# Preparation of the products of a block-wise up-projection rearranged: weight sums, taps, operands, kept tiles, transfers

## The chip, the core and the metric

The kernel runs on one core of a Trainium2 chip. The metric is the device time of one execution in microseconds (us); a kernel's time is the median of three executions. The engines are named as in the profile: PE (TensorE, matmuls), DVE (VectorE), ACT (ScalarE), POOL (GpSimd), SP (SyncE, which issues the DMA transfers). Each engine takes its instructions in the order in which the program lists them, and semaphores make one wait for another.

## The reference

One layer of a decoder for 1024 prompt positions and 8 decoded ones (1032 columns), model width 1024, feed-forward width 2816. What the change touches is the end of the mixer, the gated feed-forward block and the start of its down-projection:

```python
    x = x + m @ w_out                                   # m: merged branches
    h = rmsnorm(x, g_ffn)
    up = causal_dwconv(h @ w_up, buf, conv_f_w, conv_f_b)   # width 3, per channel
    gate, val = up[..., :D_FF], up[..., D_FF:]
    x = x + (jax.nn.gelu(gate) * val) @ w_down
```

Everything is float32; the kernel writes each matmul operand as a rounded part and a remainder (fp32r) and adds three products of such parts.

## The kernel before, in words

All activations lie with channels on the 128 partitions and the 1032 positions along the free axis. A weight tile of 128 output channels comes from memory into a `raw` or `val` tile; ACT casts it to the rounded part and DVE subtracts that from the source to get the remainder. The stage that the change touches is a list of 186 jobs, run by `run_jobs`. A job is one PE product (`product`, L1072): 24 matmuls of 128x128 by 258 columns, which is half of the contraction (four tiles of 128) for half of the positions (516 columns), three part products each.

- **Out-projection**: 32 jobs, `out_job`, two position halves times eight output tiles times two contraction halves. After each output tile DVE adds the product to x (L1124), ACT squares it (L1128), DVE adds the squares up (L1130). At the end of each half `stats` and `factors` make the norm's factor with a few small matmuls (L250, L279).
- **Up-projection**: 154 jobs, `up_job`. Gate and value channels of one row i (22 rows), split in halves of the contraction, are multiplied by the four quarters of h in seven products instead of eight: kinds m, r, p, c, q, b, z. Kinds r, p, c, q multiply sums of weight quarters; DVE makes a sum (L1243) right before ACT's cast (L973) and DVE's remainder (L978). The activations' operands are sums too: b11, b21, t1, t2, b22, t3, t4, each four tiles, made by `operand` from the normed h (norm L1167, differences L1175 and L1177, cast L235, remainder L236). Product m of row i, then p, q and z, add into one PSUM tile; r and c share another; between two of them `done` reads the intermediate value out (m L1263 or L1265, r L1267, p L1269, c L1271, q L1273, b L1275, z L1277). The b products of rows 0 to 9 come first, while the second half's operands are not there yet; in rows 2 to 9 the order is m of row i, z of row i-1, then r, p, c, q of row i. From row 10 on it is m, r, p, c, q, b, z.
- **After z**: `finish_up` convolves both halves of the row: a first tap on ACT (L1291), two taps on DVE (L1288, twice), gelu on ACT (L1309), the product of the two on DVE (L1313), and the result goes to memory (`actd`). These steps stand in `queue`.

`run_jobs` sets the order of all that, written out by the program itself (no scheduler moves it): for job n it issues the matmuls, then `done` of job n-1, then ACT's cast for job n+3 (`LOOK` = 3, `prep_hi`), then what hangs on the job, then steps from `queue` as long as the budget is positive (`SLOT` = 2.7 us less the costs, `drain`), then DVE's remainder for job n+3 (`prep_lo`), after which the next weight transfer is issued. At the end of the list the first eight results come back from memory (`fetch_act`) and are taken apart (ACT L1350, DVE L1351) for the down-projection, whose matmuls are those of `gemm` (L231).

All 16 tiles of x for the out-projection, the convolution's state and two packed weight tiles are asked for from SP before the first job.

## Time and profile before

| | |
|---|---|
| median of 3 executions | 1750.18 us (1749.72 to 1750.69) |
| profiled execution | 1752.57 us, of which the span shown is 1750.40 us |
| PE, DVE, ACT, POOL busy | 1690.7, 1138.7, 597.6, 10.5 us |
| mean granted PE clock | 0.989 of full |
| the jobs' stage | from 789.48 to 1388.36 us of the span |

The profile is one execution taken by the hardware profiler. A row of its timeline gives start, duration, engine, line, operation, tiles, and in brackets how long the engine stood idle before it and whom it waited for. Durations of one instruction overlap with the next one on the same engine: the distance of two starts is what an instruction costs there. In the rows from windows, the clock column is the share of full speed that PE was granted, 1.00 being 2.4 GHz and half of it 1.2 GHz.

### The profile page before, as it was taken

Reading aid. Unit: us, or ns where it says so; the run is one execution under the profiler, and the core shown is the slowest. Engines: PE = TensorE matmul, PEld = TensorE weight load, DVE = VectorE, ACT = ScalarE, POOL = GpSimd, SP = SyncE. Lnnn points to the kernel's source line nnn. Section 1 sums busy time; section 2 is a strip of 40 time slices with the busy share of each in tenths; the row PEclk is TensorE's granted clock in tenths of the full one; section 3 lists DMA queues with packets and bytes.
Section 4 is the critical chain, followed back from the end, with each engine's and each line's share of the span. In section 5 each row is a group of like instructions: output and inputs, shape, how many; then the busy total and the mean of one; then the engine's idle time right before and its main releaser. Section 6 shows DMA issues by size and latency. Waiting matters only on the chain.

```text
span 1750.4 us, 28104 instructions
## 1 busy us (share of the span) xinstructions
PE 1690.7 (97%) x11740; PEld 1671.6 (95%) x11740; DVE 1138.7 (65%) x1821; ACT 597.6 (34%) x944; POOL 10.5 (1%) x36
## 2 busy tenths in 40 slices
PE   7999999999999999999998898999999899999997
PEld 7999999999999999999997898999999899999997
DVE  6998978877875511554567777777777733224766
ACT  6313422211225114333334534445444522113522
POOL 0000000000000000000000000000000000000000
PEclk9999999999999999999999899999999899999998
DMA  8444332111110211117231122222222553111222
GB/s 299 143 133 126 111 114 87 54 38 55 61 39 23 73 60 56 49 62 255 101 109 54 68 76 94 73 73 73 74 97 85 212 192 116 43 53 44 101 75 92
DMA packets 72670, 163.81 MB, mean 94 GB/s; under 512 B 9056, under 2 KB 29408, under 8 KB 72544
## 3 DMA queue, kind: packets, MB, share of 16 engines
q1 hardware_dynamic: 72544, 162.02, 27.6%
q8 instruction: 92, 1.51, 0.4%
q14 instruction: 34, 0.28, 0.0%
HBM read 125.33 MB, written 32.47 MB: 90 GB/s over the span
## 4 chain that ended last, share of the span: by engine, by line
PE 80%; DVE 9%; ACT 6%; issue 3%; DMA 2%; SPq 0%; ACTq 0%; DVEq 0%
PE mm L231 58%; PE q L1072 17%; DVE wx L978 2%; DVE w L1288 1%; ACT w L1291 1%; ACT wx L973 1%; PE ps L685 1%; DVE sum L1243 1%; ACT u L235 1%; ACT w L1309 1%; PE ps L279 1%; DVE w L1167 1%; PE ps L250 1%; ACT v L930 0%; PE ps L646 0%
## 5 line engine op out<-in xcount | busy, mean ns | idle before, releaser
L231 PE MATMUL mm<-u,whi 128*128 128x344 f32 x3068 | 586.6, 321 | 1.4 <-ACT u L1277 0.7
L231 PEld LDWEIGHTS mm<-u,whi 128*128 128x128 f32 x3068 | 500.2, 188 | 3.9 <-ACT u L1277 1.0
L1072 PE MATMUL q<-u,wx 128*128 128x258 f32 x3408 | 425.5, 285 | 11.6 <-DVE wx L978 4.6
L1072 PEld LDWEIGHTS q<-u,wx 128*128 128x128 f32 x3408 | 416.6, 191 | 16.0 <-DVE wx L978 8.1
L231 PE MATMUL mm<-u,wlo 128*128 128x344 f32 x1498 | 326.9, 321 | 0.0
L235 ACT CAST whi<-raw 128x1024 fp32r<-128x1024 f32 (+2 forms) x106 | 94.1, 888 | 598.1 <-PE mm L231 512.1
L231 PEld LDWEIGHTS mm<-u,wlo 128*128 128x128 f32 x1498 | 252.1, 188 | 0.3 <-issue 0.2
L236 DVE TENSOR_TENSOR wlo<-raw,whi 128x1024 fp32r<-128x1024 f32 (+2 forms) x106 | 108.2, 1021 | 125.2 <-ACT whi L235 124.7
L1072 PE MATMUL q<-w,wx 128*128 128x258 f32 x1056 | 143.3, 294 | 24.0 <-DVE u L1273 23.3
L1072 PEld LDWEIGHTS q<-w,wx 128*128 128x128 f32 x1056 | 136.8, 199 | 27.1 <-issue 18.2
L1288 DVE SCALAR_TENSOR_TENSOR w<-u,vec,w 128x1023 f32<-128x1023 f32 x88 | 112.8, 1281 | 73.4 <-ACT w L1291 73.4
L828 DVE SCALAR_TENSOR_TENSOR u<-u,vec,u 128x1023 f32<-128x1023 f32 (+14 forms) x120 | 152.0, 1267 | 2.8
L231 PE MATMUL mm<-v,whi 128*128 128x344 f32 x552 | 103.9, 320 | 0.4 <-ACT v L866 0.4
L973 ACT CAST wx<-sum 128x512 fp32r<-128x512 f32 x66 | 40.9, 620 | 152.8 <-DVE sum L1243 142.6
L231 PEld LDWEIGHTS mm<-v,whi 128*128 128x128 f32 x552 | 90.1, 188 | 0.7 <-ACT v L866 0.7
L978 DVE TENSOR_TENSOR wx<-raw,wx 128x512 fp32r<-128x512 f32 x88 | 60.4, 687 | 27.2 <-ACT wx L973 27.2
L973 ACT CAST wx<-raw 128x512 fp32r<-128x512 f32 x88 | 53.8, 618 | 56.5 <-issue 25.5
L231 PE MATMUL mm<-w,whi 128*128 128x344 f32 (+2 forms) x360 | 72.4, 321 | 0.0
L231 PE MATMUL mm<-w,u 128*128 128x344 f32 (+2 forms) x360 | 68.2, 321 | 0.0
L978 DVE TENSOR_TENSOR wx<-sum,wx 128x512 fp32r<-128x512 f32 x66 | 45.6, 690 | 34.4 <-ACT wx L973 34.4
L1457 DVE TENSOR_TENSOR u<-u,mm 128x1032 f32<-128x1032 f32 x12 | 14.8, 1230 | 80.3 <-PE mm L231 80.3
L231 PE MATMUL mm<-v,wlo 128*128 128x344 f32 x312 | 66.3, 321 | 0.0
(309 smaller groups left out, 1754.2 us busy)
## 6 DMA issues: line engine op xcount, KB each, us to landing
raw<-in_w_in SPq DMA_DIRECT2D x44, 512.0 KB, 3.4
actd<-w SPq DMA_DIRECT2D x22, 516.0 KB, 2.9
raw<-in_w_up SPq DMA_DIRECT2D x22, 512.0 KB, 3.9
val<-in_w_up SPq DMA_DIRECT2D x22, 512.0 KB, 3.5
u<-actd SPq DMA_DIRECT2D x16, 516.0 KB, 6.2
raw<-in_w_out SPq DMA_DIRECT2D x16, 512.0 KB, 3.3
raw<-in_w_down SPq DMA_DIRECT2D x16, 448.0 KB, 3.2
u<-in_xT SPq DMA_DIRECT2D x24, 172.0 KB, 4.2
```

What stands on the lines that cost most here:

```text
L231: last[0] = pe.matmul(out[:, 0:x.shape[1]], w[i][wi], x, start=(i == 0 and p == 0), stop=(i == n - 1 and p == 2))
L235: sc.copy(hi, src)
L236: return ve.tensor_tensor(lo, src, hi.bitcast(F32), op=ALU.subtract)
L250: pe.matmul(st[0:n, c + i:c + i + 1], sq[:, o:o + n], n_inv, start=j == 0, stop=j == len(sqs) - 1)
L279: pe.matmul(r[:, j * P:j * P + n], y[0:n, i * w + j:i * w + j + 1].to_broadcast([n, P]), ident[0:n, 0:n], start=True, stop=True)
L685: pe.matmul(o, ttv[:, g], ug, start=True, stop=False)
L828: ve.scalar_tensor_tensor(o[:, d:SEQ], a[:, 0:SEQ - d], tap(i, TAPS - 1 - d), o[:, d:SEQ], op0=ALU.mult, op1=ALU.add)
L973: sc.copy(job.w[:, 0:KH * P], src)
L978: ve.tensor_tensor(job.w[:, n:2 * n], src, job.w[:, 0:n].bitcast(F32), op=ALU.subtract)
L1072: pe.matmul(ps[:, b, 0:HB], w[:, (wi * KH + k) * P:(wi * KH + k + 1) * P], xs[k][xi][:, b * HB:(b + 1) * HB], start=(start and k == 0 and ...
L1167: ve.scalar_tensor_tensor(hx(half, k0 + k), hx(half, k0 + k, xw), col("g_ffn", k0 + k), pair(rb, half), op0=ALU.mult, op1=ALU.mult)
L1288: ve.scalar_tensor_tensor(o[:, d:SEQ], u[:, 0:SEQ - d], w, o[:, d:SEQ], op0=ALU.mult, op1=ALU.add)
```

## The change

- **Weight sums one product ahead**: `prep_src` makes the DVE sum for the job after the next one to be prepared, right behind that one's cast. Sums r, p, c get a tile of their own each (three buffers) instead of adding in place.
- **Both first taps together**: the value half's first tap follows the gate half's at once on ACT, not behind the gelu.
- **Operands in stages**: a step of `operand` casts tile k on ACT and subtracts for tile k-1 on DVE.
- **Four weight tiles kept**: the last four w_out tiles (eight half tiles) of the first position half stay in SBUF for the second; their eight jobs there need no transfer, cast or remainder. `run_jobs` counts only the other jobs for its look-ahead.
- **Transfers spread out**: x comes tile by tile from within the jobs; the packed weights are asked for at job 12, the first two gate tiles at jobs 18 and 20.
- **Budgets**: `SLOT` is 2.8, and a step is taken when the budget exceeds half its cost.
- **Down-projection's first operands**: fetched in the second-last row, and taken apart one or two at a time over p, c, q, b and z of the last row (before: two each in p, c, q, b).
- Tiles of 1040 columns become 1032; the last of the early b results uses another pool.

```diff
-SLOT = 2.7
+SLOT = 2.8
+KEPT = 4
...
+    def prep_src(job):
+        if job.src is None:
+            job.src = job.prep()
+
     def prep_hi(job):
-        src = job.prep()
-        job.w = ring.tile([P, D], F32R, tag=("whi", "wlo")[n_halves[0] % 2], name=nm("wx"))
-        n_halves[0] += 1
-        sc.copy(job.w[:, 0:KH * P], src)
-        return src
+        prep_src(job)
+        job.w = job.new() if job.new else ring_half()
+        sc.copy(job.w[:, 0:KH * P], job.src)
...
-        while queue and (budget > 0 or any(q[2] == mark for q in queue)):
+        while queue and (budget > 0.5 * queue[0][0] or any(q[2] == mark for q in queue)):
...
-            nxt = jobs[n + LOOK] if n + LOOK < len(jobs) else None
+            nxt = todo[n_ready] if n_ready < min(len(todo), n_run + LOOK) else None
             if nxt:
-                src = prep_hi(nxt)
+                prep_hi(nxt)
                 budget -= nxt.prep_cost
+                n_ready += 1
+                if n_ready < len(todo):
+                    prep_src(todo[n_ready])
...
-    for half in range(2):
-        for k in range(KD):
-            sy.dma_start(pair(hw[half][k // 2], k % 2), I["xT"][:, k, half * HN:(half + 1) * HN])
...
+    fetch_x(0, range(3))
+    for j in range(KD):
+        jobs[2 * j].after.append(lambda j=j: fetch_x(0, range(3 + j, min(4 + j, KD))))
+        jobs[2 * j + 1].after.append(lambda j=j: fetch_x(1, range(j, j + 1)))
...
-                t, x = new(F32R), hx(src[0], src[1] + k)
-                ops.setdefault(name, []).append((pair(t, 0), pair(t, 1)))
-                split_into(pair(t, 0), pair(t, 1), x)
-            queue.append((cost, fn, name))
+                t = new(F32R)
+                parts_.append((pair(t, 0), pair(t, 1)))
+                sc.copy(parts_[k][0], hx(src[0], src[1] + k))
+                if k:
+                    low(k - 1)
+            queue.append((cost if k else cost - 0.7, fn, name))
+        queue.append((0.7, lambda: low(KH - 1), name))
...
             sc.activation(og[:, full], og[:, full], AF.Gelu_apprx_tanh)
-            v1()
...
         g1()
+        v1()
...
-    for n, kind in enumerate("rpcqb"):
-        up[KF - 1, kind].after.append(act_steps(2 * n, 2 if n < 4 else 0, n > 0))
+    for o, step in (((KF - 2, "b"), (3, unit3, 0)), ((KF - 1, "r"), (4, unit, 0)), ((KF - 1, "p"), (0, None, 1)),
+                    ((KF - 1, "c"), (1, unit, 1)), ((KF - 1, "q"), (0, None, 2)), ((KF - 1, "b"), (0, None, 2)),
+                    ((KF - 1, "z"), (0, None, 2))):
+        up[o].after.append(act_steps(*step))
```

Three places show how instructions move. In each, the line numbers are the kernel's own: L985, L1292, L1312, L1320, L1322, L1337, L1345, L1400 after the change are L978, L1243, L1263, L1271, L1273, L1288, L1296, L1351 before it, and on ACT L981, L1316, L1318, L1326, L1340, L1341 are L973, L1267, L1269, L1277, L1291, L1292.

First DVE in one of the rows 2 to 9, from the read of c to the first conv tap of an earlier row; `sum` and `raw` are weight sums, `wx` a part of a job's weights, `q` a PSUM tile, `u` a row's result, `w` its convolution. Before:

```order
L1271 TENSOR_TENSOR u_9473<-u_9473,q_9480 128x516
L1243 TENSOR_TENSOR sum_9543<-val_9388 128x512
L978 TENSOR_TENSOR wx_9612<-sum_9543,wx_9612 128x512
L1273 SCALAR_TENSOR_TENSOR u_9474<-q_9419,u_9474 128x516
L1243 TENSOR_TENSOR sum_9543<-sum_9543,raw_9320 128x512
L978 TENSOR_TENSOR wx_9642<-sum_9543,wx_9642 128x512
L1263 TENSOR_TENSOR u_9669<-w_8482,q_9615 128x516
L1243 TENSOR_TENSOR sum_9543<-sum_9543,raw_9320 128x512
L978 TENSOR_TENSOR wx_9673<-sum_9543,wx_9673 128x512
L1243 TENSOR_TENSOR raw_9320<-raw_9320,val_9388 128x512
L1288 SCALAR_TENSOR_TENSOR w_9702<-u_9473,vec,w_9702 128x1023
L1296 TENSOR_TENSOR w_9702<-w_9702,bf 128x8
```

After:

```order
L1320 TENSOR_TENSOR u_9447<-u_9447,q_9454 128x516
L1292 TENSOR_TENSOR sum_9587<-sum_9551,raw_9293 128x512
L985 TENSOR_TENSOR wx_9585<-sum_9551,wx_9585 128x512
L1322 SCALAR_TENSOR_TENSOR u_9448<-q_9392,u_9448 128x516
L1292 TENSOR_TENSOR sum_9618<-sum_9587,raw_9293 128x512
L985 TENSOR_TENSOR wx_9616<-sum_9587,wx_9616 128x512
L1312 TENSOR_TENSOR u_9645<-w_8449,q_9590 128x516
L1292 TENSOR_TENSOR raw_9293<-raw_9293,val_9360 128x512
L985 TENSOR_TENSOR wx_9648<-sum_9618,wx_9648 128x512
L1337 SCALAR_TENSOR_TENSOR w_9481<-u_9250,vec,w_9481 128x1023
L1345 TENSOR_TENSOR w_9481<-w_9481,bf 128x8
L985 TENSOR_TENSOR wx_9684<-raw_9293,wx_9684 128x512
```

Each sum stood right before the remainder that needs ACT's cast of it; now it stands one job earlier, and between a sum and the remainder made of it lie a read and another sum. The tap and the last remainder (of `raw`) change little in place; the tap is of the row before.

ACT from the read of z on, in such a row, before and after:

```order
L1277 ACTIVATE u_9474<-q_9419 128x516
L1291 ACTIVATE w_9702<-u_9473,vec 128x1032
L1292 COPY sv<-u_9473 128x10
L973 CAST wx_9707<-raw_9320 128x512
L1267 COPY u_9670<-q_9676 128x516
L973 CAST wx_9740<-raw_9516 128x512
L1309 ACTIVATE w_9702<-w_9702 128x1032
L1291 ACTIVATE w_9703<-u_9474,vec 128x1032
L1292 COPY sv<-u_9474 128x10
```

```order
L1326 ACTIVATE u_9448<-q_9392 128x516
L1340 ACTIVATE w_9678<-u_9447,vec 128x1032
L1341 COPY sv<-u_9447 128x10
L1340 ACTIVATE w_9679<-u_9448,vec 128x1032
L1341 COPY sv<-u_9448 128x10
L981 CAST wx_9684<-raw_9293 128x512
L1316 COPY u_9646<-q_9652 128x516
L981 CAST wx_9716<-raw_9491 128x512
L1318 COPY u_9645<-q_9590 128x516
```

The second first tap (`w_9703`) stood behind the gelu; it (`w_9679`) now stands ahead of the weight cast that follows z.

Second, DVE around the last steps of operand t2 (L1167, L1177 and L236 before are L1213, L1223 and L1197 after), from the first weight sum on. Before:

```order
L1243 TENSOR_TENSOR sum_8555<-val_8455 128x512
L1167 SCALAR_TENSOR_TENSOR w_7174<-w_7174,vec,w_7192 128x516
L1177 SCALAR_TENSOR_TENSOR w_7849<-w_7849,w_7174 128x516
L236 TENSOR_TENSOR u_8631<-w_7849,u_8631 128x516
L978 TENSOR_TENSOR wx_8627<-sum_8555,wx_8627 128x512
L1243 TENSOR_TENSOR sum_8590<-val_8526 128x512
L236 TENSOR_TENSOR u_8664<-w_7173,u_8664 128x516
L236 TENSOR_TENSOR u_8667<-w_7173,u_8667 128x516
L978 TENSOR_TENSOR wx_8662<-sum_8590,wx_8662 128x512
L1263 TENSOR_TENSOR u_8696<-w_8336,q_8635 128x516
```

After:

```order
L1292 TENSOR_TENSOR sum_8558<-val_8422 128x512
L1213 SCALAR_TENSOR_TENSOR w_7174<-w_7174,vec,w_7179 128x516
L1223 SCALAR_TENSOR_TENSOR w_7849<-w_7849,w_7174 128x516
L1197 TENSOR_TENSOR u_8526<-w_7848,u_8526 128x516
L985 TENSOR_TENSOR wx_8556<-raw_7895,wx_8556 128x512
L1292 TENSOR_TENSOR sum_8595<-val_8493 128x512
L1213 SCALAR_TENSOR_TENSOR w_7174<-w_7174,vec,w_7179 128x516
L1223 SCALAR_TENSOR_TENSOR w_7849<-w_7849,w_7174 128x516
L1197 TENSOR_TENSOR u_8562<-w_7849,u_8562 128x516
L985 TENSOR_TENSOR wx_8593<-sum_8558,wx_8593 128x512
L1292 TENSOR_TENSOR sum_8631<-sum_8558,raw_7812 128x512
```

The remainder of an operand tile (`u`) followed the difference (`w_7849`) that its cast waits for; it is now that of the tile before (`w_7848` behind a difference on `w_7849`).

Third, DVE in the last row from the remainder for b to the reads of c and q. The L1351 and L1400 rows take the down-projection's operands apart. Before:

```order
L1351 TENSOR_TENSOR u_13206<-u_13206,u_13207 128x1032
L1351 TENSOR_TENSOR u_13209<-u_13209,u_13210 128x1032
L978 TENSOR_TENSOR wx_13241<-val_12784,wx_13241 128x512
L1271 TENSOR_TENSOR u_13156<-u_13156,q_13131 128x516
L1351 TENSOR_TENSOR u_13247<-u_13247,u_13248 128x1032
L1351 TENSOR_TENSOR u_13250<-u_13250,u_13251 128x1032
L1273 SCALAR_TENSOR_TENSOR u_13157<-q_13095,u_13157 128x516
```

After:

```order
L985 TENSOR_TENSOR wx_13218<-raw_12760,wx_13218 128x512
L1400 TENSOR_TENSOR w_13079<-w_13079,u_13254 128x1032
L1361 TENSOR_TENSOR w_13141<-w_13141,w_13140 128x1032
L985 TENSOR_TENSOR wx_13252<-val_12792,wx_13252 128x512
L1320 TENSOR_TENSOR u_13177<-u_13177,q_13152 128x516
L1400 TENSOR_TENSOR w_13081<-w_13081,u_13289 128x1032
L1400 TENSOR_TENSOR u_13182<-u_13182,u_13292 128x1032
L1322 SCALAR_TENSOR_TENSOR u_13178<-q_13114,u_13178 128x516
```

Two of the steps still stand between the reads of c and q; two others, which stood ahead of z's remainder, are one now.

## Rows read from the trace of the kernel before

**Rows 1.** The windows of the jobs' stage: start and end, length, busy time of PE, PE's weight loads, DVE, ACT and POOL with their instructions, granted clock, share and rate of DMA. The first and the last window reach a little over the stage's ends.

```profile
789.00:860.00 71.00, 69.06 (x569) 68.30 (x568) 33.16 (x57) 21.38 (x38) 2.77 (x5) 1.00 0.53 188
860.00:950.00 90.00, 85.42 (x681) 82.32 (x680) 61.52 (x103) 37.84 (x70) 0.10 (x1) 1.00 0.22 79
950.00:1000.00 50.00, 40.56 (x293) 39.00 (x292) 38.66 (x56) 22.74 (x37) 0.00 (x0) 0.90 0.24 85
1000.00:1145.00 145.00, 132.89 (x1063) 131.36 (x1062) 105.11 (x146) 65.31 (x109) 0.00 (x0) 0.98 0.22 77
1145.00:1370.00 225.00, 224.57 (x1858) 223.77 (x1858) 169.01 (x234) 109.49 (x179) 0.00 (x0) 1.00 0.23 83
1370.00:1389.00 19.00, 11.24 (x68) 10.56 (x68) 13.30 (x14) 7.69 (x9) 0.00 (x0) 0.73 0.76 281
```

**Rows 2.** The waits of PE over the whole span: who waited, for whom, total us, times, longest.

```profile
PE q L1072 <- DVE u L1273: 23.3, 10, 6.7
...
PE q L1072 <- DVE wx L978: 4.6, 9, 0.8
...
PE q L1072 <- ACT wx L973: 1.9, 1, 1.9
```

**Rows 3.** From the chain of work that ended last: start, us, what. The L250 and L279 pieces are the small matmuls of the first half's `stats` and `factors`; the last piece is PE's longest run of products without a wait.

```profile
843.99 1.11 PE q L250 x12
...
851.07 1.71 PE q L279 x12
...
1162.80 194.56 PE q L1072 x1608
```

**Rows 4.** PE's timeline in the stage: its first products, those that the text speaks of, and the first `gemm` of the down-projection.

```profile
789.48 17.45 PE L1072 MATMUL q<-u,wx 128*128 128x258 f32 x144
...
961.74 4.32 PE L1072 MATMUL q<-w,wx 128*128 128x258 f32 x20 [4.11 <-DVE u L1273]
...
980.02 8.27 PE L1072 MATMUL q<-u,wx 128*128 128x258 f32 x48 [4.24 <-DVE u L1263]
...
1014.25 3.15 PE L1072 MATMUL q<-w,wx 128*128 128x258 f32 x24 [1.82 <-DVE u L1273]
...
1053.10 4.62 PE L1072 MATMUL q<-w,wx 128*128 128x258 f32 x24 [1.80 <-DVE u L1273]
...
1131.70 4.62 PE L1072 MATMUL q<-w,wx 128*128 128x258 f32 x24 [1.76 <-DVE u L1273]
...
1382.16 5.50 PE L1072 MATMUL q<-w,wx 128*128 128x258 f32 x24 [6.69 <-DVE u L1273]
1388.36 1.23 PE L231 MATMUL mm<-u,whi 128*128 128x344 f32 x6 [0.69 <-ACT u L1277]
```

**Rows 5.** DVE's timeline within one of the rows 2 to 9.

```profile
1025.26 1.28 DVE L1288 SCALAR_TENSOR_TENSOR w<-u,vec,w 128x1023 f32<-128x1023 f32 x1 [2.33 <-ACT w L1291]
1026.46 0.16 DVE L1296 TENSOR_TENSOR w<-w,bf 128x8 f32<-128x8 f32 x1
...
1028.45 1.23 DVE L1313 TENSOR_TENSOR w<-w,w 128x1032 f32<-128x1032 f32 x1
1029.60 0.69 DVE L978 TENSOR_TENSOR wx<-val,wx 128x512 fp32r<-128x512 f32 x1
1030.20 0.68 DVE L1271 TENSOR_TENSOR u<-u,q 128x516 f32<-128x516 f32 x1
1030.80 0.69 DVE L1243 TENSOR_TENSOR sum<-val 128x512 f32<-128x512 f32 x1
1032.23 0.69 DVE L978 TENSOR_TENSOR wx<-sum,wx 128x512 fp32r<-128x512 f32 x1 [0.74 <-ACT wx L973]
1032.84 0.69 DVE L1273 SCALAR_TENSOR_TENSOR u<-q,u 128x516 f32<-128x516 f32 x1
```

**Rows 6.** ACT's timeline in the same row, from the read of z on.

```profile
1018.00 0.60 ACT L1277 ACTIVATE u<-q 128x516 f32<-128x516 f32 x1
1018.49 1.24 ACT L1291 ACTIVATE w<-u,vec 128x1032 f32<-128x1032 f32 x1
...
1019.72 0.62 ACT L973 CAST wx<-raw 128x512 fp32r<-128x512 f32 x1
...
1023.99 1.24 ACT L1291 ACTIVATE w<-u,vec 128x1032 f32<-128x1032 f32 x1
```

**Rows 7.** DVE's timeline where the operands t2 and b22 are made.

```profile
934.69 0.69 DVE L1243 TENSOR_TENSOR sum<-sum,raw 128x512 f32<-128x512 f32 x1
936.67 0.70 DVE L236 TENSOR_TENSOR u<-w,u 128x516 fp32r<-128x516 f32 x1 [1.29 <-ACT u L235]
937.28 0.68 DVE L978 TENSOR_TENSOR wx<-sum,wx 128x512 fp32r<-128x512 f32 x1
```

**Rows 8.** SP's timeline early in the out-projection: the convolution's state and a w_out tile.

```profile
795.91 0.33 SPq L1203 DMA_DIRECT2D bf<-in_st_f  x1
...
803.45 0.39 SPq L993 DMA_DIRECT2D raw<-in_w_out  x1
```

**Rows 9.** DVE's timeline in the last row, a step of L1351 and the read of q.

```profile
1378.09 1.23 DVE L1351 TENSOR_TENSOR u<-u,u 128x1032 fp32r<-128x1032 f32 x1 [1.84 <-ACT u L1350]
...
1381.33 0.69 DVE L1273 SCALAR_TENSOR_TENSOR u<-q,u 128x516 f32<-128x516 f32 x1
```

**Rows 10.** ACT's timeline there.

```profile
1377.00 1.05 ACT L1350 CAST u<-u 128x1032 fp32r<-128x1032 f32 x1 [5.87 <-DMA u<-actd]
```

More of the change, by code (lines that the diff above doesn't have):

```diff
@@ L1006, in done @@
             out_done(half, j, out_ps.pop((half, j)))
-        job = Job(lambda: half_slab(out_raw[half * KD + j], sub), 0.7, run, done if sub else None, 0.7)
-        if sub and half * KD + j + 2 < 2 * KD:
+        n = half * KD + j
+        job = Job(lambda: half_slab(out_raw[n], sub), 0.7, run, done if sub else None, 0.7)
+        if j >= KD - KEPT:
+            if half:
+                job.kept = out_kept[j, sub]
+            else:
+                job.new, out_kept[j, sub] = (lambda: unit(F32R)), job
+        if sub and n + 2 < 2 * KD - KEPT:
             job.fetch.append(fetch_out)
@@ L1031, in build @@
                 for job in jobs[0:2]:
-                    prep_lo(job, prep_hi(job))
+                    prep_hi(job)
+                    prep_lo(job)
         ve.tensor_tensor(v3(s2), v3(s2), pv(ps), op=ALU.mult)
@@ L1084, in run_jobs @@
     def run_jobs():
-        for job in jobs[0:LOOK]:
+        todo = [job for job in jobs if job.kept is None]
+        n_run = 0
+        for job in todo[0:LOOK]:
             if job.w is None:
-                prep_lo(job, prep_hi(job))
+                prep_hi(job)
+                prep_lo(job)
+        n_ready = LOOK
         for n, job in enumerate(jobs):
@@ L1091, in run_jobs @@
                 drain(0, job.needs)
-            job.run(job.w)
+            if job.kept is None:
+                n_run += 1
+                job.run(job.w)
+            else:
+                job.run(job.kept.w)
             budget = SLOT
@@ L1235, in prep @@
                 return half_slab(packs[i // 2], i % 2)
-            if i not in sums_w:
-                sums_w[i] = ring3.tile([P, KH * P], F32, tag="sum", name=nm("sum"))
-            a11, a12, a21, a22 = (half_slab(t[i], e) for t in (gates, vals) for e in range(2))
-            s = sums_w[i]
+            a11, a12 = half_slab(gates[i], 0), half_slab(gates[i], 1)
+            a21, a22 = (half_slab(vals[i], e) for e in range(2)) if i in vals else (None, None)
             if kind in "mbz":
                 return {"m": a11, "b": a12, "z": a22}[kind]
-            out, x, y = {"r": (s, a21, a22), "p": (s, s, a11), "c": (s, s, a12), "q": (a11, a11, a21)}[kind]
+            if kind == "q":
+                out, x, y = a11, a11, a21
+            else:
+                out = ring3.tile([P, KH * P], F32, tag="sum", name=nm("sum"), bufs=3)
+                x, y = {"r": (a21, a22), "p": (sums_w.get(i), a11), "c": (sums_w.get(i), a12)}[kind]
+                sums_w[i] = out
             ve.tensor_tensor(out, x, y, op=ALU.add)
@@ L1327, in build @@
         up[i, kind] = up_job(i, kind)
-    jobs[-3].fetch.append(lambda: fetch_gate(0))
-    jobs[-1].fetch.append(lambda: fetch_gate(1))
+    for i in range(2):
+        jobs[n_half + 2 * (KD - KEPT + i) - 3].fetch.append(lambda i=i: fetch_gate(i))
     for n in range(2, EARLY // 2):
@@ L1371, in build @@
     plan.reverse()
-    up[KF - 1, "z"].after.append(ahead)
-    fetch_pack(0)
-    fetch_pack(1)
+    up[KF - 1, "c"].after.append(fetch)
+    up[KF - 1, "b"].after.append(ahead)
+    jobs[n_half - 4].after.append(lambda: (fetch_pack(0), fetch_pack(1)))
     with tc.manual_schedule():
```

49 lines of the change are left out of this document (32 added, 17 removed).

## The prediction

> **What bounds the kernel now.** I read the windows of the stage first, since the share of busy time is a mean over stages, then PE's list of waits, PE's timeline around each wait, and last DVE's and ACT's timelines at the places that PE waits for. The change touches the stage of 186 products, from 789.48 to 1388.36: 598.88 us [rows 4]. What PE needs there without any wait comes from its longest run: 1608 matmuls in 194.56 us, 0.1210 us each, so 2.904 us for a product of 24 [rows 3]. 186 products are 540.1 us; the small matmuls of `stats` and `factors`, twice 1.11 + 1.71, add 5.65 [rows 3]. The rest, 598.88 - 545.75 = 53.1 us, is all that the change can win here, as the matmuls stay the same ones.
>
> The windows say where those 53.1 us lie. Length less PE's busy time is 1.94, 4.58, 9.44, 12.11, 0.43 and 7.76 us [rows 1], 36.3 us together. In three of them the granted clock is under 1.00 (0.90, 0.98, 0.73): products right behind a wait run at a mix of 1.2 and 2.4 GHz. PE's timeline shows what that costs against the same number of matmuls at full speed (3.15 for 24): 1.9 at 961.74, 2.5 at 980.02 (48 matmuls), 1.5 each at 1053.10 and 1131.70, 2.35 at 1382.16 [rows 4], 9.7 us. Most of the remaining 7 us is the 0.25 us by which 24 matmuls after a short wait take longer than 2.90, 3.15 against it, some 25 times. From 1162.80 to 1357 PE never waits [rows 3] and nothing can be won.
>
> **The change part by part.** *Spread-out transfers.* The first window's idle 1.94 us [rows 1] is one wait, for a weight cast [rows 2]. The w_out tile that this cast needs was issued at 803.45, behind the x tiles and, at 795.91, the convolution's state [rows 8]. With three x tiles ahead of the first job, and the others one per job, the tile has the queue nearly to itself: gain 1.94 + 0.25, remainder 0 (at most the old 2.2, if the transfer itself is what lasts).
>
> *Sums one ahead, operands in stages.* In 860 to 1000 PE waits for remainders made by DVE. DVE's rows show why it is late while it is busy only 0.77 of the time from 950 to 1000 (38.66 of 50 [rows 1]): the sum of 934.69 is followed by an idle 1.29 us, waiting for ACT's cast, before the operand's remainder at 936.67 and the weight's at 937.28 [rows 7]. Sum, cast and remainder of one job, then cast and remainder of an operand tile, go back and forth between two engines, and a product's share of this takes 3.2 to 3.8 us instead of 2.9. With the sum made a job earlier ACT can cast at once, and with the remainder of tile k-1 behind the cast of tile k DVE has no cast to wait for. What is left per product is four or five half-wide DVE operations at a distance of 0.60 [rows 5]: 2.4 to 3.0 us, under or about 2.904. The two long waits (4.11 before 961.74, 4.24 before 980.02 [rows 4]) are the sum of that lag, met by the first reads of q and m. I expect 0.7 us to be left of the 14 us idle there, because two rows' first taps and reads of m and q come close together in rows 0 and 1; bounds 0 and 3, the 3 being two paired taps on ACT (twice 1.24 [rows 6]) and a half-wide read.
>
> *Rows 2 to 9.* Seven waits like the one of 1.82 at 1014.25 (1.80 at 1053.10, 1.76 at 1131.70 [rows 4]) make a row 19.4 us long, (1053.10 - 1014.25)/2, where six products need 17.42. PE's z of row i-1 waits for DVE's read of q (the 1273 entry, 23.3 us in ten waits, less the 4.11 and 6.69 that stand elsewhere [rows 2, 4]). On DVE the read waits its turn behind two waits for ACT: 2.33 before the first tap at 1025.26, because the value half's tap on ACT comes only behind the gelu (1023.99 [rows 6]), and 0.74 before the remainder at 1032.23, right behind its own sum of 1030.80 [rows 5]. After the change the sum of q's successor stands a job ahead, and the tap is there some 5 us earlier. DVE's work in a row is then 13 half-wide operations at 0.60 (7.9), four taps at 1.20, two corrections of 0.07 and a product of 1.15 [rows 5]: 14.0 us. One wait is added: the weight cast behind z now stands on ACT behind the read of z and both taps, 0.49 + 1.23 + 1.23 + 0.62 = 3.6 us [rows 6], some 3.8 behind z with the start of the read, while DVE has a tap and a correction to do, 1.27 us; that leaves 2.5 us of waiting, and 16.5 us for the row. It is under 17.42 by 0.9, so I take the seven waits as gone: 12.0 idle, 3.0 of clock and seven times 0.25 come back, 17 us. The remainder lies between 0 and that 17; I take 0, by the rows. From row 10 on a row has seven products, 20.3 us, and DVE about 17; no new wait. The tap that moves on ACT also moves ahead of the read of r and of two casts; PE has three products prepared by then (`LOOK`).
>
> *The end.* The last z waits 6.69 us and runs slowly [rows 4]: the read of q at 1381.33 stands behind steps that take the down-projection's operands apart [rows 9], and ACT's cast for one of them had waited 5.87 for its transfer [rows 10]. About 10.6 us of the 53.1 lie here, with 0.69 before the first `gemm`. The change asks for these operands a row earlier, so the transfer's wait goes; but between the starts of the last row and of z DVE still takes five of eight apart, 1.15 to 1.23 us each [rows 9], beside seven half-wide operations, the last taps and a product. Counted from the row's start T along the new order: first subtraction done at T+7.0, two taps and a remainder to 10.1, the second to 11.2, a product to 12.35, z's remainder 12.95, read of c 13.55, two more subtractions 15.85, read of q 16.45. PE could start z at T+14.5 (five products); it starts at 16.55, a wait of 2.05. After z come two more, a weight step and the reads: `gemm` some 1.15 behind z's end. With 0.25 twice and half of the 2.35 that the slow clock cost (two of the seven 1.8-us waits were followed by a slow product), 4.9 us stay; bounds 1.2 and 10.6.
>
> *Kept tiles.* Eight jobs lose a cast of 0.62 [rows 6], a remainder of 0.69 [rows 5], and four transfers go. In the second half of the out-projection this shortens ACT and DVE; what short waits on remainders lie there [rows 2] is in the 4.58. Apart from that it costs and gives nothing: PE's products cover it, and without that cover each job would be worth 1.3. Tile width, `SLOT` and the half-cost rule: nothing on PE, a step of 1.2 us earlier or later.
>
> **Sum.** 53.1 less what stays: 0 + 0.7 + 0 + 4.9, and about 1.0 for short waits that I do not see (an estimate: four of the 0.25). 46.5 us gained, so the span falls from 1750.40 to 1703.9 and the execution from 1752.57 to 1706.1; that execution lies 2.39 (0.14%) over the median, so on the median 1750.18 - 46.5 = **1703.7**.
>
> **Two rules beside it.** The seven equal waits go for a read of the PSUM tile that z itself adds into [rows 2, 4]. The Trainium skill (Perfetto Trace Analysis, Optimization Strategy) says that the same gap again and again on the engine that should be saturated can mean too little SBUF or PSUM for the next tile. The change adds no PSUM tile, so by that rule the gaps stay and the time would be about 1721; the rows, where the tile waited for is an old one, speak for 1704. ACT's cast at 1019.72 starts when the tap ahead of it ends [rows 6], though nothing ties it to the tap. The Trainium skill (TensorE: Matmul & The Clock Gate, on the array's architectural detail) says that ACT and DVE take their queues strictly in order and that only TensorE moves something ahead, its weight loads; the trace agrees, and this speaks against putting both taps ahead of the cast: by it alone 1776, the slower rival.
>
> **The rivals.** *The seven waits remain* (slack 0.9 of 17.4 is small, and DVE's added wait of 2.5 is worked out, not read): 17 us are not won, 1721. For it: the PSUM tile is read by the same operation at nearly the same place. Against: both ACT waits ahead of it go. *The end stays*: 10.6 instead of 4.9, 1709. *Half the operand waits stay* (the ping-pong moves to ACT): some 10 us, 1714. *The change does not do what it says*: the three buffers of the sums are freed late, so a sum waits for a remainder and DVE is where it was: 1747 to 1753. *Slower*: the paired taps. In rows 2 to 21, 20 of them, the cast behind z comes up to 3.6 us later; if PE waited for the whole of it each time, that would be 72 us against the 46.5: 1776. It decides from the point where DVE's row with its wait is longer than PE's: 17.4 us early, 20.3 later; it turns the sign only above 2.5 us in each row. Against it are three prepared jobs, 8.7 us of PE work, between that cast and its use.
>
> **How the numbers follow.** Forecast 1704, its own range 1698 (only the 1.0 stays) to 1712 (3 and 10.6 stay beside the 1.0): 0.68. Seven waits 0.10, end 0.08, half the operands 0.05, no effect 0.04, slower 0.05. Range 1698 to 1722, which leaves out the last two and a little. Faster by over 0.2% (3.5 us, about what a measurement can tell from no change) 0.91, within it 0.04, slower 0.05.
>
> **What would show it.** Right: a stage of about 552 us; PE's list of waits without ten entries for the read of q; windows with as good as no idle time and a clock of 1.00 from 790 to the last row; rows 2 to 9 of 17.4 us; one wait of about 2 before the last z and one of about 1 before `gemm`; no wait for the third w_out tile; the steady product still 2.904. Wrong: z waiting for the read of q in every early row, or PE waiting for a cast right behind two taps, or a last z that waits 6 us though its transfers are in.

## The result and the profile after

The changed kernel takes 1710.61 us (median of 4 executions, 1709.36 to 1713.67) beside 1749.95 for the kernel before (1748.25 to 1750.69): a ratio of 0.9779, with a 95% interval from 0.9762 to 0.9796. The gain is 39 us, where 46.5 were forecast. The profiled execution took 1710.39 us with a span of 1708.2.

PE's windows of the jobs' stage, cut at places like those of [rows 1], with the same columns:

```profile
790.00:860.00 70.00, 70.00 (x579) 69.63 (x579) 36.79 (x62) 22.90 (x40) 3.11 (x5) 1.00 0.59 200
860.00:950.00 90.00, 90.00 (x746) 89.58 (x744) 65.57 (x113) 38.54 (x68) 0.10 (x1) 1.00 0.20 72
950.00:1000.00 50.00, 47.29 (x388) 46.74 (x387) 38.92 (x55) 26.98 (x43) 0.00 (x0) 1.00 0.18 64
1000.00:1130.00 130.00, 127.32 (x1049) 126.30 (x1048) 107.29 (x150) 64.32 (x106) 0.00 (x0) 1.00 0.25 90
1130.00:1330.00 200.00, 200.00 (x1666) 200.00 (x1665) 146.08 (x206) 95.50 (x159) 0.00 (x0) 1.00 0.29 97
1330.00:1347.00 17.00, 14.07 (x104) 13.60 (x103) 16.37 (x18) 11.46 (x14) 0.00 (x0) 0.90 0.55 188
```

PE is busy for the whole of the first two windows, where it had stood idle for 6.5 us; the granted clock is 1.00 up to the last row. Idle time is left in three windows: 2.71 us between 950 and 1000, 2.68 between 1000 and 1130, and 2.93 at the end. The list of PE's waits (who waited, for whom, total us, times, longest) says what for:

```profile
PE q L1089 <- ACT u L1316: 5.4, 7, 2.2
PE q L1089 <- DVE u L1322: 2.2, 1, 2.2
...
PE mm L232 <- ACT u L1326: 0.7, 1, 0.7
```

The ten waits for the read of q (L1322, L1273 before [rows 2]) are one, that of the last z. Another entry has grown: seven waits for L1316, ACT's read of r (L1267 before), where the list of the kernel before has one:

```profile
PE q L1072 <- ACT u L1267: 0.4, 1, 0.4
```

PE's timeline after the change, from the first product of the stage to the first matmul of the down-projection:

```profile
790.76 23.26 PE L1089 MATMUL q<-u,wx 128*128 128x258 f32 x192
...
964.76 3.15 PE L1089 MATMUL q<-u,wx 128*128 128x258 f32 x24 [2.23 <-ACT u L1316]
...
982.84 3.15 PE L1089 MATMUL q<-u,wx 128*128 128x258 f32 x24 [0.48 <-ACT u L1316]
...
1019.27 3.16 PE L1089 MATMUL q<-u,wx 128*128 128x258 f32 x24 [0.48 <-ACT u L1316]
...
1037.35 3.15 PE L1089 MATMUL q<-u,wx 128*128 128x258 f32 x24 [0.48 <-ACT u L1316]
...
1341.52 4.38 PE L1089 MATMUL q<-w,wx 128*128 128x258 f32 x24 [2.24 <-DVE u L1322]
1346.59 0.75 PE L232 MATMUL mm<-u,whi 128*128 128x344 f32 x3 [0.69 <-ACT u L1326]
```

The stage runs from 790.76 to 1346.59, 555.83 us, where it took 598.88 [rows 4]. That is 43.05 less. A row in the early part takes 18.08 us (1037.35 - 1019.27): some 17.4 for its products, 0.48 of wait (0.76 in one row) and 0.2 for the start after it. The last z waits 2.24 and the down-projection's first matmul 0.69.

Where the wait of 0.48 comes from is read on ACT and DVE in such a row. ACT, from the read of z:

```profile
1013.03 0.60 ACT L1326 ACTIVATE u<-q 128x516 f32<-128x516 f32 x1 [2.23 <-PE q L1089]
1013.53 1.24 ACT L1340 ACTIVATE w<-u,vec 128x1032 f32<-128x1032 f32 x1
...
1014.76 1.25 ACT L1340 ACTIVATE w<-u,vec 128x1032 f32<-128x1032 f32 x1
...
1016.00 0.62 ACT L981 CAST wx<-raw 128x512 fp32r<-128x512 f32 x1
1018.62 0.59 ACT L1316 COPY u<-q 128x516 f32<-128x516 f32 x1 [2.01 <-DVE w L1337]
```

DVE, from the read of q to the conv tap that ACT's read of r waits for:

```profile
1007.82 0.69 DVE L1322 SCALAR_TENSOR_TENSOR u<-q,u 128x516 f32<-128x516 f32 x1
...
1011.95 1.28 DVE L1337 SCALAR_TENSOR_TENSOR w<-u,vec,w 128x1023 f32<-128x1023 f32 x1
...
1016.65 0.69 DVE L985 TENSOR_TENSOR wx<-raw,wx 128x512 fp32r<-128x512 f32 x1 [3.35 <-ACT wx L981]
1017.26 1.28 DVE L1337 SCALAR_TENSOR_TENSOR w<-u,vec,w 128x1022 f32<-128x1022 f32 x1
```

ACT reads z, makes both first taps (1013.53, 1014.76) and only then the cast at 1016.00. DVE waits 3.35 us for that cast at 1016.65, and its next conv tap, at 1017.26, is late by as much. That tap is the last reader of a tile of the row two before, and ACT's read of r goes into this tile's place: it waits 2.01 us for the tap, starts at 1018.62, and PE's c, which adds into the PSUM tile that r's read must leave first, starts at 1019.27.

### The profile page after: what moved, and what is told of

Its sections match the earlier page's. It is cut to its first block, busy times and chain, and to the rows that moved or that the text cites. A ratio compares the mean times of both kernels' runs of the same rounds, so it can differ in the third digit from the quotient of the medians.

```text
span 1708.2 us, 28051 instructions
## 1 busy us (share of the span) xinstructions
PE 1678.5 (98%) x11740; PEld 1664.9 (97%) x11740; DVE 1129.7 (66%) x1813; ACT 592.4 (35%) x936; POOL 10.9 (1%) x36
## 4 chain that ended last, share of the span: by engine, by line
PE 93%; ACT 4%; DVE 2%; DMA 1%; issue 1%; SPq 0%; DVEq 0%; ACTq 0%
PE mm L232 59%; PE q L1089 29%; ACT w L1340 1%; PE ps L686 1%; PE ps L280 1%; DMA ped<-z 1%; DVE w L1337 0%; ACT v L931 0%; PE ps L251 0%; PE ps L647 0%; PE ps L687 0%; PE ps L232 0%; PE ps L801 0%; PE ps L659 0%; DVE wx L985 0%
## 5 line engine op out<-in xcount | busy, mean ns | idle before, releaser
L232 PE MATMUL mm<-u,whi 128*128 128x344 f32 x2996 | 576.3, 321 | 1.3 <-ACT u L1326 0.7
L232 PEld LDWEIGHTS mm<-u,whi 128*128 128x128 f32 x2996 | 489.9, 188 | 3.9 <-ACT u L1326 1.0
L1089 PE MATMUL q<-u,wx 128*128 128x258 f32 x3024 | 373.7, 283 | 5.4 <-ACT u L1316 5.4
L1089 PEld LDWEIGHTS q<-u,wx 128*128 128x128 f32 x3024 | 367.5, 189 | 6.9 <-ACT u L1316 6.8
L236 ACT CAST whi<-raw 128x1024 fp32r<-128x1024 f32 (+2 forms) x106 | 94.1, 887 | 602.8 <-PE mm L232 501.6
L1089 PE MATMUL q<-w,wx 128*128 128x258 f32 x1056 | 135.4, 285 | 2.2 <-DVE u L1322 2.2
L1089 PEld LDWEIGHTS q<-w,wx 128*128 128x128 f32 x1056 | 131.3, 191 | 2.6 <-issue 2.4
L1337 DVE SCALAR_TENSOR_TENSOR w<-u,vec,w 128x1023 f32<-128x1023 f32 x88 | 112.5, 1280 | 22.0 <-ACT w L1340 22.0
L232 PE MATMUL mm<-w,whi 128*128 128x344 f32 (+2 forms) x432 | 87.5, 320 | 0.0
L985 DVE TENSOR_TENSOR wx<-raw,wx 128x512 fp32r<-128x512 f32 x72 | 50.3, 699 | 40.0 <-ACT wx L981 40.0
L232 PEld LDWEIGHTS mm<-w,whi 128*128 128x128 f32 x432 | 71.5, 188 | 0.2
L981 ACT CAST wx<-sum 128x512 fp32r<-128x512 f32 x66 | 40.8, 618 | 67.4 <-PE q L1089 61.4
L232 PEld LDWEIGHTS mm<-w,u 128*128 128x128 f32 x360 | 58.1, 188 | 1.0
```

The lines of the kernel that those rows point to most:

```text
L232: last[0] = pe.matmul(out[:, 0:x.shape[1]], w[i][wi], x, start=(i == 0 and p == 0), stop=(i == n - 1 and p == 2))
L236: sc.copy(hi, src)
L981: sc.copy(job.w[:, 0:KH * P], job.src)
L985: ve.tensor_tensor(job.w[:, n:2 * n], job.src, job.w[:, 0:n].bitcast(F32), op=ALU.subtract)
L1089: pe.matmul(ps[:, b, 0:HB], w[:, (wi * KH + k) * P:(wi * KH + k + 1) * P], xs[k][xi][:, b * HB:(b + 1) * HB], start=(start and k == 0 and ...
L1337: ve.scalar_tensor_tensor(o[:, d:SEQ], u[:, 0:SEQ - d], w, o[:, d:SEQ], op0=ALU.mult, op1=ALU.add)
```

## The experiments

All kernels are the changed one with the edit shown, unless said otherwise. The stage's length is the distance from its first product to the first matmul of the down-projection in each kernel's trace. Ratios are to the kernel before, run beside each.

| kernel | median us | ratio (95%) | stage us |
|---|---|---|---|
| before | 1750 to 1752 | 1 | 598.88 |
| changed | 1710.61 | 0.9779 (0.9762 to 0.9796) | 555.83 |
| e4, tap behind the cast | 1705.12 | 0.9740 (0.9725 to 0.9755) | 550.91 |
| e1, tap behind the gelu | 1711.33 | 0.9775 (0.9758 to 0.9791) | 554.37 |
| e2, sums not ahead | 1713.01 | 0.9784 (0.9770 to 0.9799) | 556.81 |
| e3, operands whole | 1721.71 | 0.9837 (0.9822 to 0.9851) | 566.48 |
| e5, e1 and e2 together | 1715.74 | 0.9796 (0.9780 to 0.9811) | 556.84 |
| e8, old budgets | 1703.25 | 0.9723 (0.9705 to 0.9741) | 548.17 |
| e9, e8 and e1 together | 1719.29 | 0.9821 (0.9804 to 0.9838) | 563.77 |
| e10, e8 and e2 together | 1707.88 | 0.9750 (0.9735 to 0.9765) | 551.41 |
| e11, nothing kept, x at once | 1714.67 | 0.9792 (0.9778 to 0.9807) | 558.64 |
| e6, before with narrow tiles | 1755.97 | 1.0023 (1.0013 to 1.0034) | 598.39 |
| e7, wide tiles up to the stage | 1711.20 | 0.9771 (0.9757 to 0.9786) | 554.84 |
| e12, old budgets, later operands | 1702.14 | 0.9719 (0.9703 to 0.9735) | 546.03 |

The executions of one kernel lie up to 5.6 us apart, so where two intervals overlap the stages are compared. A stage is read from one execution of each kernel; so where two stages differ by 1 or 2 us only, the lists of waits carry the argument.

**Tap behind the cast (e4).** The first question was whether the paired taps make the new wait.

```diff
         g1()
-        v1()
+        queue.insert(0, (0.0, v1, "conv"))
```

> The value half's first tap goes behind the weight cast that follows z on ACT, instead of ahead of it; all else as in the changed kernel. Theory A (what stays of the old 53 us is the slower rival in small: the cast behind z stands on ACT behind two taps, DVE waits 3.35 us for it in each of the rows 3 to 8, its next conv tap frees a row's tile late, ACT's read of r starts late, and PE's c waits 0.48): the cast comes 1.23 us earlier, DVE's wait is about 2.1, the seven waits of PE for the read of r (5.4 us, and 1.7 of slower starts) are gone, about 1704. Rival B (DVE's row is full whatever waits in it, or c waits for its own weights): waits of the same size for the same or another instruction, 1710 or 1711.

Measured: 1705.12, stage 550.91. PE's waits in the stage:

```profile
PE q L1089 <- ACT u L1316: 2.3, 1, 2.3
...
PE q L1089 <- DVE u L1322: 1.7, 1, 1.7
...
PE mm L232 <- DVE u L1324: 0.9, 1, 0.9
```

Of the seven waits for r one is left, the one of row 2 (2.3). DVE waits 2.11 us for the cast, where it waited 3.35 and about 2.1 was expected:

```profile
1015.92 0.69 DVE L985 TENSOR_TENSOR wx<-raw,wx 128x512 fp32r<-128x512 f32 x1 [2.11 <-ACT wx L981]
```

Theory A holds for rows 3 to 8: the order on ACT, one tap of 1.23 us ahead of one cast, made PE wait in rows in which DVE is busy 0.83 of the time (107.29 of 130 us in the windows above). The stage is 4.9 us shorter, 3.3 of it up to the start of the last b (542.2 us against 545.5) and 1.6 at the end, where the last z waits 1.7 instead of 2.2 and runs at full clock.

**Tap behind the gelu (e1), sums not ahead (e2), operands whole (e3).** Each takes one of the three named parts back.

```diff
             sc.activation(og[:, full], og[:, full], AF.Gelu_apprx_tanh)
+            v1()
...
         g1()
-        v1()
```

> The value half's first tap goes back behind the gelu on ACT; DVE's order stays that of the changed kernel. If the pairing of the taps was needed to take the seven waits for the read of q away (as the prediction added it up, a DVE wait of 2.33 us in each row), they come back in part: 7 waits of 1 us or more, 1718 or more. If the weight sums a product ahead were enough, the waits for the read of q stay away, and with only one tap ahead of the cast behind z the waits for the read of r go too: 1703 to 1706.

Measured: 1711.33, stage 554.37. In rows 3 to 9 neither waits for q nor for r are there, only the one for r of row 2 (2.1): up to the start of the last b the stage is 3.7 us shorter than the changed kernel's (541.7 against 545.5). Against that stand the end (the last z waits 2.9 and the down-projection 2.1) and one wait of 0.9 in row 10. ACT's timeline shows where the tap now stands:

```profile
1005.18 1.07 ACT L1358 ACTIVATE w<-w 128x1032 f32<-128x1032 f32 x1 [2.52 <-DVE w L1337]
1006.15 1.23 ACT L1340 ACTIVATE w<-u,vec 128x1032 f32<-128x1032 f32 x1
...
1007.37 1.14 ACT L981 CAST wx<-sum 128x512 fp32r<-128x512 f32 x2
```

The tap at 1006.15 holds up the cast of a weight sum (1007.37) by 1.23 us, and DVE waits 1.14 for it ahead of the read of q. So the wait that pairing was to remove is partly there, and yet PE does not feel it. The time lay above what the second theory gave, 1703 to 1706, by the end of the stage and by what follows it: from the stage's end to the end of the span it is 363.8 us, where the changed kernel takes 361.6; from 1350 to 1360 the granted clock is 0.93, in the changed kernel 1.00.

```diff
-                if n_ready < len(todo):
-                    prep_src(todo[n_ready])
```

> Each weight sum is made right ahead of its own cast again, in a tile of its own; taps, operands and the rest as in the changed kernel. If the sums are the main part: in rows 2 to 9 DVE waits some four times 0.75 us more in a row, on top of 18.1 us, so a row is about 20 us and some 20 us come back there, and of the waits where the operands are made about 10: 1740 (1730 to 1750). If the taps and the operands' order did it, 1711 to 1715.

Measured: 1713.01, stage 556.81, 1.0 more than the changed kernel's, and that at the end (up to the last b 545.6 against 545.5). It is the second of the two outcomes named, and it goes against the prediction's reasoning, in which the sums were the main part. DVE's timeline in a row:

```profile
1009.48 0.69 DVE L985 TENSOR_TENSOR wx<-sum,wx 128x512 fp32r<-128x512 f32 x1 [0.74 <-ACT wx L981]
...
1012.14 0.69 DVE L985 TENSOR_TENSOR wx<-sum,wx 128x512 fp32r<-128x512 f32 x1 [0.76 <-ACT wx L981]
...
1014.80 0.69 DVE L985 TENSOR_TENSOR wx<-sum,wx 128x512 fp32r<-128x512 f32 x1 [0.76 <-ACT wx L981]
...
1018.68 0.69 DVE L985 TENSOR_TENSOR wx<-raw,wx 128x512 fp32r<-128x512 f32 x1 [1.31 <-ACT wx L981]
```

The waits for casts are back, 0.74 to 0.76 at 1009.48, 1012.14 and 1014.80. But only the first lies ahead of the read of q, which follows it at 1010.09, and PE is not ready for that one yet: z starts at 1011.96, right behind the product before it.

```profile
1011.96 3.06 PE L1089 MATMUL q<-w,wx 128*128 128x258 f32 x24
```

The other two merely shorten the wait for the cast behind z, 1.31 at 1018.68 instead of 3.35. Waits in a chain that is tied to PE at one point do not add up.

```diff
-                if k:
-                    low(k - 1)
-            queue.append((cost if k else cost - 0.7, fn, name))
-        queue.append((0.7, lambda: low(KH - 1), name))
+                low(k)
+            queue.append((cost, fn, name))
```

> A step that makes an operand subtracts for the tile that it has just cast, as before the change; sums, taps and the rest as in the changed kernel. DVE then waits 0.69 us for ACT's cast in each of some 28 steps. If the order of the operands matters by itself: about 3.4 us for a product where DVE has 2.7 of work, waits of PE for remainders between 900 and 960, 5 to 14 us, 1716 to 1724. If the sums ahead were enough there: 1711.

Measured: 1721.71, stage 566.48, 10.7 more. PE's waits:

```profile
PE q L1089 <- DVE u L1320: 5.9, 2, 3.6
PE q L1089 <- ACT u L1314: 5.0, 7, 1.8
...
PE q L1089 <- DVE wx L985: 1.9, 3, 0.9
```

Besides those for r (and that of the last z, 2.3) there are three waits for remainders (L985) and one of 3.6 for the first read of q, all between 920 and 956, and in the window from 945 to 968 the granted clock is 0.78. The operands' order carries 10.7 us of what was won there; with that order in place the sums carry next to nothing (e2). What the sums would do without it was not tried.

**The budgets (e5, e8, e9, e10).** With neither tap nor sums needed when taken back singly, something else might keep the seven waits for q away. In DVE's order after the change the tap near z is that of the row before: the conv steps lag. The budgets were suspected of that.

> Both are undone at once: each sum right ahead of its own cast, and the value half's first tap behind the gelu. The new budgets (2.8, and a step when the budget exceeds half its cost) stay. Theory A (the budgets let the conv taps lag by a row's part, so that between the cast behind z and the read of q DVE has only one sum's wait of 0.74 and one of 1.1 left, which the slack of about 1.4 takes, and this keeps the seven waits for q away): at most 0.5 us for a row, 1710 to 1716. Rival B (sums ahead or paired taps each suffice, and one of them must be there): the seven waits of 1.8 us are back with their slower starts, 1722 to 1728.

Measured: 1715.74, stage 556.84. The edit is those of e1 and e2 together. No wait for q in rows 3 to 9, and none for r in them either, only that of row 2 (2.8) and two short ones from row 10 on (0.3 and 0.7): theory A. The end is longer than the changed kernel's, as in e1 (3.4 ahead of the last z, 2.1 ahead of the down-projection).

```diff
-SLOT = 2.8
+SLOT = 2.7
...
-        while queue and (budget > 0.5 * queue[0][0] or any(q[2] == mark for q in queue)):
+        while queue and (budget > 0 or any(q[2] == mark for q in queue)):
```

> SLOT is 2.7 again and a step is taken while the budget is positive; all other parts of the change stay. The taps of a row then stand again in the same row's part on DVE. Theory A (three parts each take the seven waits away, and the lag of the taps that the new budgets bring is what makes ACT's read of r late, since a row's tile comes free later): from z's end the read of q is done at about 14.1 us, with 14.5 until PE needs it, so no waits for q, and none for the read of r: 1703 to 1706. Rival B (the new budgets alone keep the seven waits away): waits for q of 1 us or more in rows 2 to 9, 1715 or more. Rival C (budgets cost nothing, as the prediction had it): 1710 to 1711, with the waits for r as they are.

Measured: 1703.25, stage 548.17. PE's waits in the stage:

```profile
PE mm L232 <- ACT u L1326: 1.7, 1, 1.7
PE q L1089 <- DVE u L1322: 1.6, 2, 1.0
```

The seven waits for r are gone, that of row 2 too, and those for q did not come back: theory A, and the best of the single edits. The edit takes `SLOT` and the half-cost rule back together; which of the two makes the lag was not tried. On ACT the cast behind both taps (1014.34 in this kernel) is as late as before, but the read of r follows at once, since the tap that frees its tile was made in the row before:

```profile
1014.34 0.62 ACT L981 CAST wx<-raw 128x512 fp32r<-128x512 f32 x1
1014.86 0.58 ACT L1316 COPY u<-q 128x516 f32<-128x516 f32 x1
```

With the old budgets the other two parts can be weighed, by this edit with that of e1 and with that of e2:

> Old budgets, and the value half's first tap behind the gelu: of the three parts that could hold the rows 2 to 9, only the sums one product ahead are left. By the old trace one sum's wait of 0.74 lies between z and the read of q, so if waits add up the seven waits go from 1.8 to about 1.1 us and the time is 1711 to 1716; if the sums were the main cause, as the prediction had it, no waits for q and 1703 to 1706.

> Old budgets, and each sum right ahead of its own cast: of the three only the paired taps are left. They take 2.33 us of DVE's waiting away between z and the read of q, where PE waited 1.8: if waits add up, 0 to 0.4 us for a row and 1705 to 1710; if the sums were the main cause, waits for q of about 1 us, 1715 or more.

Measured: 1719.29 without pairing (stage 563.77, 15.6 more than old budgets alone) and 1707.88 without the sums ahead (551.41, 3.2 more). PE's waits without pairing:

```profile
PE q L1089 <- DVE u L1322: 8.7, 9, 1.7
...
PE q L1089 <- DVE u L1312: 3.3, 1, 3.3
```

The waits are back with sums ahead as the only help: six for q of 1.03 to 1.05 us in rows 3 to 8, and one of 1.04 behind them that the profile puts down to ACT's read of m. So the expectation's size for sums alone was right (1.1 for a wait) and the time above it, because row 2 and the end lost as well (3.3 for the read of m in row 2, with 48 slow matmuls behind it). Pairing alone leaves 0.3 to 0.9 us in a row, and its list has:

```profile
PE q L1089 <- DVE u L1320: 3.0, 4, 1.6
```

**Nothing kept, x at once (e11).**

```diff
-KEPT = 4
+KEPT = 0
...
-    fetch_x(0, range(3))
-    for j in range(KD):
-        jobs[2 * j].after.append(lambda j=j: fetch_x(0, range(3 + j, min(4 + j, KD))))
-        jobs[2 * j + 1].after.append(lambda j=j: fetch_x(1, range(j, j + 1)))
+    fetch_x(0, range(KD))
+    fetch_x(1, range(KD))
...
-    jobs[n_half - 4].after.append(lambda: (fetch_pack(0), fetch_pack(1)))
+    fetch_pack(0)
+    fetch_pack(1)
```

> No weight tiles are kept, and x and the packed weights are asked for at once ahead of the first job, as before the change; all else as in the changed kernel. By the prediction the one wait near 808 us comes back, 1.94 us and 0.25 of a slower start, and the eight casts and remainders cost nothing beside PE: 1713, and no other wait of PE up to 900 us. If the kept tiles matter, short waits for remainders between 865 and 880 come back as well: 1714 or more. If neither matters: 1711.

Measured: 1714.67, stage 558.64, 2.8 more. PE's timeline from the first product on:

```profile
792.12 17.49 PE L1089 MATMUL q<-u,wx 128*128 128x258 f32 x144
811.72 35.21 PE L1089 MATMUL q<-u,wx 128*128 128x258 f32 x288 [2.10 <-ACT wx L981]
...
855.63 37.86 PE L1089 MATMUL q<-u,wx 128*128 128x258 f32 x312
```

The wait of the kernel before is back, 2.10 us ahead of 811.72, and no other: from 855.63 the products run without one to the second half's norm. The kept tiles gave nothing that PE feels.

**Tile width (e6, e7).** Ahead of the stage the change touches no instruction, and yet the stage starts later: the 4476 matmuls of 344 columns there stand a little further apart in the changed kernel and in all its variants.

```diff
-UW = 1040
+UW = 1032
```

> The kernel before with the one constant UW at 1032 instead of 1040. In every run of the changed kernel and its variants the 1580 matmuls up to 690 us, which the change does not touch, start 157.2 ns apart, in the kernel before 156.5, some 3 us over 4400 matmuls. Theory A (the tiles' width, and so their places in SBUF, set this): 157.2 ns, and 1752 to 1753 beside the 1750 of the kernel before. Rival B (something else in the program): 156.5 ns and no difference.

> The changed kernel with tiles of 1040 columns again in the two pools that serve the mixer (the others stay at 1032). Theory A (the width of the tiles that these matmuls read sets their distance): 156.5 ns and 1707 to 1708. Rival B (not the width, or not these tiles): 157.2 ns and 1710 to 1711.

In e7 the edit makes the tiles of the pools `units0` and `units2` UW + 8 wide. Windows of 230 us without a wait, from the kernel before, then from that with narrow tiles (e6), then from e7; the figure behind PE's busy time counts matmuls:

```profile
450.00:680.00 230.00, 230.00 (x1472) 229.27 (x1471) 116.86 (x146) 57.77 (x81) 0.00 (x0) 1.00 0.15 49
```

```profile
450.00:680.00 230.00, 230.00 (x1466) 229.27 (x1465) 118.53 (x147) 58.10 (x82) 0.00 (x0) 1.00 0.14 48
```

```profile
450.00:680.00 230.00, 230.00 (x1466) 229.27 (x1465) 118.52 (x147) 58.11 (x82) 0.00 (x0) 1.00 0.15 48
```

1472 matmuls with tiles of 1040 columns, 1466 with 1032, by one constant alone: 156.5 and 157.2 ns between starts (the counts take in matmuls that reach over the window's ends). The time went to 1755.97, 1.0023 of the kernel before. The width costs some 3 us ahead of the stage: from the first matmul of the kernel to the stage 783.3 us against 780.4. In e7 the count stays at 1466, so wide tiles in those two pools alone do not bring it back. Most matmuls of this window read tiles named u, of another pool; a run with only those wide was not made, and which tiles do it, and why, stays open.

**Old budgets and later operands (e12).** The budgets of e8, with less for DVE and ACT to do ahead of the last z's start and end.

```diff
-                    ((KF - 1, "c"), (1, unit, 1)), ((KF - 1, "q"), (0, None, 2)), ((KF - 1, "b"), (0, None, 2)),
-                    ((KF - 1, "z"), (0, None, 2))):
+                    ((KF - 1, "c"), (1, unit, 1)), ((KF - 1, "q"), (0, None, 1)), ((KF - 1, "b"), (0, None, 2))):
...
-    up[KF - 1, "b"].after.append(ahead)
+    up[KF - 1, "z"].after.append(ahead)
...
         jobs[-1].done()
+        take_apart(3)
```

> Old budgets (with all else of the change), and in the last row one operand fewer is taken apart ahead of the read of q, none between b and z, three behind the read of z, with the first weight tiles of the down-projection behind them. With old budgets alone the last z waited 1.03 and starts slowly (1.17 in all), and the first matmul of the down-projection came 1.9 late, since ACT's read of z stood behind four casts of 1.05. If DVE's and ACT's order there is the cause: no wait for the last z, and 0.7 to 1.2 ahead of the down-projection: 1701 to 1702 where old budgets alone gave 1703. If the transfer of the weights sets that start: 1703.

Measured: 1702.14, stage 546.03, 2.1 shorter than with old budgets alone. PE's timeline at the end:

```profile
1335.11 3.11 PE L1089 MATMUL q<-w,wx 128*128 128x258 f32 x24
1338.90 0.74 PE L232 MATMUL mm<-u,whi 128*128 128x344 f32 x3 [0.69 <-ACT u L1327]
```

The last z starts without a wait and the down-projection 0.69 behind it, so the order on the two engines was the cause. The time, 1702.14 beside 1703.25, cannot be told apart by itself; beside the changed kernel's 0.9779 the 0.9719 can.

## Why the prediction was right, and where it was off

The direction held, and so did the main mechanism: what PE could win was read rightly as some 53 us of waits, most of them for DVE, and 43 of them went. The forecast of 1704 was 7 us under the time, for the reason under 1 and for those named behind the list.

1. **The budgets.** "Tile width, `SLOT` and the half-cost rule: nothing on PE" is the step that failed. The new budgets make the conv taps lag by a part of a row, a tile comes free late, and c waits for ACT's read of r: 0.48 to 0.76 us and 0.2 of a slower start in six rows, 2.23 and 0.25 in row 2. By e8 the budgets cost 7.7 us of the stage, 1.5 of them at its end. The prediction had the pieces (3.6 us for the cast behind both taps, 2.5 of waiting on DVE, measured 3.35) and made of them a slower rival of 72 us; what came is this rival at a tenth of its price, along a way that it did not name, through the tile that the tap frees. Lag and paired taps do it together: in rows 3 to 8 the waits go with either (e8, e4).
2. **The seven waits.** That they go was right; why was only partly so. With the old budgets pairing the taps is worth 15.6 us and the sums ahead 3.2 (e9, e10); with the new ones neither is needed to keep these waits away (e5). The prediction added up waits that lie between different points of PE's row. Only what lies between the cast behind z and the read of q counts there, and what comes later is taken out of the next wait.
3. **The operands.** Some 14 us of idle time went as forecast; the 2.7 us left in these windows, where 0.7 were expected, are c's waits of rows 2 and 3 (2.23 and 0.48), counted under 1. It was the order of cast and remainder that did it (10.7 by e3), not the sums.
4. **The first stall** went and comes back with the old transfers: by e11 the stretch from the first product to the first small matmul takes 54.65 us instead of 52.03, 2.10 of the difference being the wait; 1.94 and 0.25 were forecast. **The end** kept 4.5 us (2.24 of wait, 1.2 for the lower clock on z, 0.69 and two starts) where 4.9 were expected, the gap before z 2.24 against 2.05. **The kept tiles** cost and gave nothing. These three were right.

One sign on the prediction's list did not come: a steady product of 2.904 us. Seven products, a row from row 10 on, took 20.30 us before and take 20.20 after, 2.886 each:

```profile
1194.76 11.80 PE L1072 MATMUL q<-u,wx 128*128 128x258 f32 x96
...
1215.06 11.80 PE L1072 MATMUL q<-u,wx 128*128 128x258 f32 x96
```

```profile
1160.19 11.72 PE L1089 MATMUL q<-u,wx 128*128 128x258 f32 x96
...
1180.39 11.72 PE L1089 MATMUL q<-u,wx 128*128 128x258 f32 x96
```

In the old trace one start in nearly every such row stands 0.22 us behind the one before instead of 0.12, too little to be listed as a wait. It stands there too in the two other kernels with neither sums ahead nor paired taps (e5, e6), and in none that has one of them. So some of what the sum took as PE's need, about 1 us, could be won as well.

That the stage came within 3.4 us of the forecast (598.88 - 46.5 = 552.4 against 555.83) is partly luck. Without the cost of the budgets it is 548.17 (e8), 4.2 under the forecast: the 0.7 and 1.0 kept for waits, the end and PE's need were put too high, and that hid more than half of the 7.7.

Beside the stage there are two more terms, 0.8 and 2.9 of the 7 us. The narrow tiles, the other half of the step under 1, cost about 3 us ahead of it (e6), part of which an earlier first matmul hides in the profiled execution (7.21 us from the start, where it was 9.12). And the execution that the sum was made against lay 2.39 us over its median; the whole gain was carried over to the median, though the trace of the changed kernel lies on its own. 43.05 in the stage, 1.28 lost ahead of it and some 0.5 gained behind it make the 42.2 by which the two spans differ, and 39.3 the medians.

Of the rules weighed, the one on bubbles (the Trainium skill, Perfetto Trace Analysis, Optimization Strategy) missed for the old gaps: they went without one more PSUM tile. For the new gaps of 0.48 us it holds: ACT's read of r waits for the place of a tile that is still read, 2.01 us at 1018.62. The strict order of ACT (the Trainium skill, TensorE: Matmul & The Clock Gate, on the array's architectural detail) showed as expected: the cast at 1016.00 stands right behind two taps, and with one of them moved behind it (e4) DVE's wait for the cast fell from 3.35 to 2.11.

## What to carry to other kernels

Cost a constant that sets an order by the order that it makes: a row that "changes little in place" but belongs to the iteration before is a lag, and a lag keeps a buffer. Ahead of adding up waits on a helper engine, mark the points at which it is tied to the main engine; only the waits between two such points move the end. When several edits are meant for one stall, undo them singly and in pairs: here three of them covered for one another, and one cost more than it gave.
